# The last tile of a row normalisation: four single row multiplications on VectorE, or one with broadcast factors

## The chip, the cores and the metric

The kernel runs on one core of a Trainium2 chip. The metric is the device time of one execution, in microseconds (us). Before the change it is 316.5 us, the median of three runs (316.45, 316.50, 316.88).

## The reference

The input x has 32 x 512 rows of 1024 fp32 numbers. Each row is divided by the sum of its absolute values:

```python
def reference(x: np.ndarray) -> np.ndarray:
    sums = np.sum(np.abs(x), axis=-1, keepdims=True)
    return (x / (sums + 1e-8)).astype(np.float32)
```

Input and output have 67.1 MB each, so 134.2 MB have to be moved between HBM and the core's memory. Beside that there is little to compute: one reduction and one multiplication for each element.

## The kernel before, in words

The 16384 rows are spread over 128 partitions, 128 rows to each. They are worked off in eleven tiles, numbered 0 to 10. A tile holds R = 12 rows of 1024 numbers for every partition (48 KB a partition, 6144 KB in all), but the last, tile 10, only 8 rows (32 KB a partition, 4096 KB). There are BUFS = 4 buffers; tile i takes the buffer of tile i - 4 once that one is stored.

For every tile the program does four things, in this order:

- `load(i)` (line 87) is a DMA issued on SyncE's queue (SP in the profile; its packets are on q1).
- `normalize` (lines 45 to 73) computes in place. VectorE (DVE) sums the absolute values of all rows in one instruction (line 47), adds 1e-8 (line 54) and takes the reciprocals (line 56): `inv` has one factor for each row. Then the rows are multiplied by their factors, and here the rows are divided among three kinds of instruction. The first `kv` rows go to VectorE in one multiplication of two tensors, where the second is `inv` broadcast along each row (line 58). The next `kt` rows go to VectorE too, one instruction for each row, with the row's factor as a scalar per partition (line 65). The remaining `ks` rows go to ScalarE (ACT), one activation each (line 68).
- `store(i)` (line 97) is a DMA issued on ScalarE's queue (q10). It waits until VectorE's and ScalarE's rows of the tile are done. Tile 0 and tile 8 are stored in two parts, all others in one.
- `load(i + 4)` for the buffer that will come free.

The table `split` on line 76 gives `(kt, ks)` for some tiles; all the others have (0, 0), which means that VectorE does all rows with the one multiplication of line 58. The schedule is manual: each engine carries out its instructions in the order in which the program issues them, and the waits between engines are put in where data or buffers require them.

The end of the program matters here. Tile 9 has (0, 2): ten rows by line 58 on VectorE, two on ScalarE, then its store of 6144 KB. Tile 10 has (4, 4): `kv` is 0, four rows by line 65 on VectorE and four on ScalarE at the same time, then the last store, of 4096 KB. Both stores are cut into packets of a whole partition's rows (`WHOLE`, line 95): 48 KB for tile 9, 32 KB for tile 10. After that only SyncE's final wait for the stores remains.

Of the kernel before, what the change touches and what calls it, by code (L numbers as in the profile page):

```python
# [1 line left out]

# [4 lines left out]

FP32 = mybir.dt.float32
EPS = 1e-8


@with_exitstack
def kernel(
    ctx: ExitStack,
    tc: tile.TileContext,
    x: bass.AP,
    out: bass.AP,
):
    nc = tc.nc
    P = nc.NUM_PARTITIONS  # L20

    x_flat = x.flatten_outer_dims()
    out_flat = out.flatten_outer_dims()
    n, d = x_flat.shape

    R = 12
    BUFS = 4
    HEAD = 32
    per_partition = n // P
    assert n % P == 0 and (per_partition - HEAD) % R == 0  # L30
    rows = [R] * ((per_partition - HEAD) // R + 2) + [HEAD - 2 * R]

    def piece(flat, i):
        head = flat[: P * HEAD, :].rearrange("(p r) d -> p r d", p=P)
        if i < 2:
            return head[:, R * i : R * (i + 1), :]
        if i == len(rows) - 1:
            return head[:, 2 * R :, :]
        a = P * (HEAD + R * (i - 2))
        return flat[a : a + P * R, :].rearrange("(p r) d -> p r d", p=P)  # L40

    sbuf = ctx.enter_context(tc.tile_pool(name="sbuf", bufs=BUFS))
    stats = ctx.enter_context(tc.tile_pool(name="stats", bufs=len(rows)))

    def normalize(x_tile, k, kv, kt):
        s = stats.tile([P, R], FP32)
        nc.vector.tensor_reduce(  # L47
            out=s[:, :k],
            in_=x_tile[:, :k, :],
            axis=mybir.AxisListType.X,  # L50
            op=mybir.AluOpType.add,
            apply_absolute_value=True,
        )
        nc.vector.tensor_scalar_add(out=s[:, :k], in0=s[:, :k], scalar1=EPS)  # L54
        inv = stats.tile([P, R], FP32)
        nc.vector.reciprocal(out=inv[:, :k], in_=s[:, :k])  # L56
        if kv:
            nc.vector.tensor_mul(  # L58
                out=x_tile[:, :kv, :],
                in0=x_tile[:, :kv, :],  # L60
                in1=inv[:, :kv].unsqueeze(2).to_broadcast([P, kv, d]),
            )
        for r in range(kv, kv + kt):
            row = x_tile[:, r, :]
            nc.vector.tensor_scalar_mul(out=row, in0=row, scalar1=inv[:, r : r + 1])  # L65
        for r in range(kv + kt, k):
            row = x_tile[:, r, :]
            nc.scalar.activation(  # L68
                out=row,
                in_=row,  # L70
                func=mybir.ActivationFunctionType.Copy,
                scale=inv[:, r : r + 1],
            )

    last = len(rows) - 1
    split = {0: (3, 4), 1: (0, 3), 2: (0, 3), last - 1: (0, 2), last: (4, 4)}

    tiles = {}

    HALF, WHOLE = 24576, 49152
    FIRST = 3

    def load(i):
        x_tile = tiles[i] = sbuf.tile([P, R, d], FP32, name="x_tile")
        nc.sync.dma_start(out=x_tile[:, : rows[i], :], in_=piece(x_flat, i), max_dma_last_dim=WHOLE if i < 2 else HALF)  # L87

    def store(i):
        if i == 0:  # L90
            parts = [(0, FIRST, 4 * d), (FIRST, R, WHOLE)]
        elif i == last - 2:
            parts = [(0, R // 2, HALF), (R // 2, R, HALF)]
        else:
            parts = [(0, rows[i], WHOLE if i >= last - 1 else HALF)]
        for a, b, size in parts:
            nc.scalar.dma_start(
                out=piece(out_flat, i)[:, a:b, :],
                in_=tiles[i][:, a:b, :],
                max_dma_last_dim=size,  # L100
            )

    def compute(i):
        k = rows[i]
        kt, ks = split.get(i, (0, 0))
        normalize(tiles[i], k, k - kt - ks, kt)

    with tc.manual_schedule():
        for i in range(BUFS):
            load(i)  # L110
        for i in range(len(rows)):
            compute(i)
            store(i)
            if i + BUFS < len(rows):
                load(i + BUFS)


# [1 line left out]
_INS = ['x']  # L119
_OUTS = [((32, 512, 1024), 'float32')]  # L120


# [23 lines left out]
```

## Time and profile before

| what | value |
|---|---|
| time, median of three runs | 316.5 us (316.45 to 316.88) |
| the profiled execution | 316.77 us |
| its span, from the first to the last instruction | 315.2 us |
| VectorE busy | 260.6 us, 83% |
| ScalarE busy | 18.5 us, 6% |
| moved by DMA | 134.22 MB, 426 GB/s over the span |
| line 65 (single rows on VectorE) | 7 instructions, 749 ns each |
| line 58 (broadcast multiplication on VectorE) | 10 instructions of four widths |
| line 68 (single rows on ScalarE) | 16 instructions, 1138 ns each |

All times in the views are counted from the start of the span. The timeline's columns are the start, the duration of the whole group, the engine, the line, the operation, what it writes and reads, the shapes and the number of instructions; a "q" behind an engine's name is its instruction queue, where DMAs are issued. In the groups the columns after the bar are the busy us and the mean ns of one instruction, then the idle time before them. In the windows the columns are the stretch, its length, busy time and instructions of VectorE, ScalarE and GpSimd, the granted clock of TensorE (not used here), the mean busy share of the 16 DMA engines, and GB/s. A packet is counted in the window in which it starts. In the 40 slices each digit is a share in tenths; a slice is 7.9 us.

### The profile page before, as it was taken

How to read it: one execution, taken by the hardware profiler on the slowest of the kernel's cores; microseconds unless marked ns; L12 is line 12 of the kernel's file. 1: busy time of each engine (PE TensorE's matmuls, PEld its weight loads, DVE VectorE, ACT ScalarE, POOL GpSimd, SP SyncE). 2: the span in 40 equal slices, each digit the busy share in tenths (PEclk: the TensorE clock that was granted, in tenths of full speed). 3: DMA queues.
4: the chain of work that ended last, by engine and by line, in shares of the span. 5: the costliest groups of instructions: out<-in, count | busy, mean ns of one | idle time of the engine just before them, and what ended most of it. 6: DMA issues, size and time to landing. Idle time of an engine off the chain costs nothing.

```text
span 315.2 us, 172 instructions
## 1 busy us (share of the span) xinstructions
DVE 260.6 (83%) x50; ACT 18.5 (6%) x17; POOL 0.2 (0%) x4
## 2 busy tenths in 40 slices
DVE  0079999999999999989996997999699969999000
ACT  0010503004000000000000000000000000203200
POOL 0000000000000000000000000000000000000000
DMA  8999999999999999999999999999999999999997
GB/s 318 480 399 412 437 407 464 411 436 413 415 446 437 415 446 437 415 449 434 415 449 437 412 449 437 412 449 437 415 446 437 415 437 434 432 428 496 399 408 324
DMA packets 5761, 134.22 MB, mean 426 GB/s; under 512 B 385, under 2 KB 385, under 8 KB 769
## 3 DMA queue, kind: packets, MB, share of 16 engines
q1 hardware_dynamic: 2736, 67.11, 49.8%
q10 hardware_dynamic: 3024, 67.11, 49.4%
q14 instruction: 1, 0.00, 0.0%
HBM read 67.11 MB, written 67.11 MB: 426 GB/s over the span
## 4 chain that ended last, share of the span: by engine, by line
DVE 40%; DMA 33%; another core or an unknown queue 18%; ACT 1%; issue 0%; SPq 0%
DVE s L47 23%; DMA x_tile<-in_x_dram 17%; DMA out_dram<-x_tile 16%; DVE x_tile L58 15%; ACT x_tile L68 1%; DVE x_tile L65 1%; DVE inv L56 0%; DVE s L54 0%; SPq L87 0%
## 5 line engine op out<-in xcount | busy, mean ns | idle before, releaser
L47 DVE TENSOR_REDUCE s<-x_tile 128x12 f32<-128x12288 f32 (+1 forms) x11 | 138.2, 12562 | 29.8 <-DMA x_tile<-in_x_dram 29.8
L58 DVE TENSOR_TENSOR x_tile<-x_tile,inv 128x12288 f32<-128x12288 f32 (+3 forms) x10 | 113.6, 11358 | 0.5
L68 ACT ACTIVATE x_tile<-x_tile,inv 128x1024 f32<-128x1024 f32 x16 | 17.2, 1138 | 256.9 <-DVE inv L56 256.9
L65 DVE TENSOR_SCALAR x_tile<-x_tile,inv 128x1024 f32<-128x1024 f32 x7 | 4.8, 749 | 0.0
L56 DVE RECIPROCAL inv<-s 128x12 f32<-128x12 f32 (+1 forms) x11 | 2.5, 226 | 0.4
L68 ACT ACT_TABLE_LOAD x1 | 1.3, 1283 | 17.8 <-DMA x_tile<-in_x_dram 17.8
L54 DVE TENSOR_SCALAR s<-s 128x12 f32<-128x12 f32 (+1 forms) x11 | 1.9, 174 | 0.4
L130 POOL MEMSET const-bfloat16-1.0<- 128x1 bf16 x1 | 0.1, 101 | 0.0
L130 POOL MEMSET const-uint8-127<- 128x1 uint8 x1 | 0.1, 101 | 0.0
L130 POOL MEMSET const-float32-0.0<- 128x1 f32 x1 | 0.1, 98 | 0.2 <-issue 0.2
L130 POOL MEMSET const-float32-1.0<- 128x1 f32 x1 | 0.1, 98 | 0.0
## 6 DMA issues: line engine op xcount, KB each, us to landing
x_tile<-in_x_dram SPq DMA_DIRECT2D x10, 6144.0 KB, 36.9
out_dram<-x_tile ACTq DMA_DIRECT2D x8, 6144.0 KB, 49.1
out_dram<-x_tile ACTq DMA_DIRECT2D x2, 3072.0 KB, 33.4
out_dram<-x_tile ACTq DMA_DIRECT2D x1, 4608.0 KB, 37.9
x_tile<-in_x_dram SPq DMA_DIRECT2D x1, 4096.0 KB, 32.2
out_dram<-x_tile ACTq DMA_DIRECT2D x1, 4096.0 KB, 20.9
out_dram<-x_tile ACTq DMA_DIRECT2D x1, 1536.0 KB, 29.3
```

The costliest lines, as they stand in the source:

```text
L47: nc.vector.tensor_reduce(out=s[:, :k], in_=x_tile[:, :k, :], axis=mybir.AxisListType.X, op=mybir.AluOpType.add, apply_absolute_value=True,)
L54: nc.vector.tensor_scalar_add(out=s[:, :k], in0=s[:, :k], scalar1=EPS)
L56: nc.vector.reciprocal(out=inv[:, :k], in_=s[:, :k])
L58: nc.vector.tensor_mul(out=x_tile[:, :kv, :], in0=x_tile[:, :kv, :], in1=inv[:, :kv].unsqueeze(2).to_broadcast([P, kv, d]),)
L65: nc.vector.tensor_scalar_mul(out=row, in0=row, scalar1=inv[:, r : r + 1])
L68: nc.scalar.activation(out=row, in_=row, func=mybir.ActivationFunctionType.Copy, scale=inv[:, r : r + 1],)
L130: nc = _bacc.Bacc("TRN2", target_bir_lowering=False, num_devices=1)
```

## The change

One entry of the table changes: tile 10 has (0, 4) in place of (4, 4).

```diff
-    split = {0: (3, 4), 1: (0, 3), 2: (0, 3), last - 1: (0, 2), last: (4, 4)}
+    split = {0: (3, 4), 1: (0, 3), 2: (0, 3), last - 1: (0, 2), last: (0, 4)}
```

With 8 rows in the tile, `kv` = 8 - 0 - 4 becomes 4 and `kt` becomes 0. So VectorE's four rows of tile 10 are multiplied by one instruction of line 58, over 4096 columns, with the four factors broadcast along the rows, and the four instructions of line 65 over 1024 columns each are gone. ScalarE's four rows, the store and all other tiles are as they were.

## The prediction

> **What bounds the kernel now.** I began with the page: its header, the engines, the 40 slices and the packet total.
>
> ```profile
> span 315.2 us, 172 instructions
> ## 1 busy us (share of the span) xinstructions
> DVE 260.6 (83%) x50; ACT 18.5 (6%) x17; POOL 0.2 (0%) x4
> ...
> DVE  0079999999999999989996997999699969999000
> ...
> DMA  8999999999999999999999999999999999999997
> ...
> DMA packets 5761, 134.22 MB, mean 426 GB/s; under 512 B 385, under 2 KB 385, under 8 KB 769
> ```
>
> VectorE is busy for 83% of the span, but it has slices below 9 and ends three slices (24 us) before the span does. The transfers leave a slice below 9 only at the two ends. 134.22 MB at the 432 GB/s that the DMA view gives for 20:290 is 311 us, out of 315.2. So the bound is the transfers; VectorE matters only where it makes them run dry.
>
> The page's chain of waits names VectorE first (40%). It ends with ScalarE's last activation at 293.22 us and does not follow the store behind it, so it can't say what sets the end. I therefore went to the timeline of the end, where the change lies:
>
> ```profile
> 268.95 10.82 DVE L58 TENSOR_TENSOR x_tile<-x_tile,inv 128x10240 f32<-128x10240 f32 x1
> 279.79 8.69 DVE L47 TENSOR_REDUCE s<-x_tile 128x8 f32<-128x8192 f32 x1
> 279.85 0.34 ACTq L97 DMA_DIRECT2D out_dram<-x_tile  x1
> ...
> 288.96 4.27 ACT L68 ACTIVATE x_tile<-x_tile,inv 128x1024 f32<-128x1024 f32 x4 [17.82 <-DVE inv L56]
> 288.96 2.74 DVE L65 TENSOR_SCALAR x_tile<-x_tile,inv 128x1024 f32<-128x1024 f32 x4
> 293.25 0.34 ACTq L97 DMA_DIRECT2D out_dram<-x_tile  x1
> ```
>
> The four multiplications that the change replaces end at 291.70 (288.96 + 2.74), ScalarE's four rows at 293.23. The last store waits for both and is issued at 293.25: ScalarE's rows release it. What does it meet in its queue? Two answers of the DMA view follow, for 293.6:303.5 and for 303.5:315.2:
>
> ```profile
> DMA packets 80, 3.93 MB, mean 397 GB/s; under 512 B 0, under 2 KB 0, under 8 KB 0
> ...
> q10 hardware_dynamic: 80, 3.93, 91.7%
> ```
> ```profile
> DMA packets 160, 4.19 MB, mean 358 GB/s; under 512 B 32, under 2 KB 32, under 8 KB 32
> ...
> q10 hardware_dynamic: 160, 4.19, 83.1%
> ```
>
> The last store has 4096 KB, which is 4.19 MB: all of it starts after 303.5 us. The 80 packets before are of 3.93 / 80 = 49 KB, the size of the store of tile 9, which was issued at 279.85 and lands 24.6 us later, at 304.5 by the same view. So the last store waits behind tile 9's for about 303.5 - 293.25 = 10.2 us, with its instruction long done. It then takes the rest: the page's row of issues has it land 20.9 us after its issue, at 314.15, and the span ends 1.0 us later.
>
> **The change, part by part.** *Removed:* four multiplications of 128x1024 on line 65, 749 ns each by the page. They start about 0.66 us apart, so together they take 2.74 us, not 4 x 0.749. *Added:* one multiplication of 128x4096 on line 58. The trace has no such width; the groups by form have four others:
>
> ```profile
> L58 DVE TENSOR_TENSOR x_tile<-x_tile,inv 128x12288 f32<-128x12288 f32 x6 | 77.8, 12959 | 0.4
> L58 DVE TENSOR_TENSOR x_tile<-x_tile,inv 128x9216 f32<-128x9216 f32 x2 | 19.5, 9758 | 0.1
> ...
> L58 DVE TENSOR_TENSOR x_tile<-x_tile,inv 128x10240 f32<-128x10240 f32 x1 | 10.8, 10825 | 0.0
> ...
> L58 DVE TENSOR_TENSOR x_tile<-x_tile,inv 128x5120 f32<-128x5120 f32 x1 | 5.5, 5491 | 0.0
> ```
>
> They lie on one line: (12959 - 5491) / 7168 = 1.042 ns per column, and 5491 - 5120 x 1.042 = 157 ns fixed. For 4096 columns that is 4268 + 157 = 4.42 us. As bounds I keep 2.74 us (it costs what the four did) and 5.49 us (no cheaper than the 5120 columns); the line is the nearest, so I take 4.42.
>
> *Moved:* nothing else. Built, the changed program differs in this one place; the other instructions, their order and the two waits of the last store (on VectorE, on ScalarE) are the same.
>
> The sum: VectorE ends at 288.96 + 4.42 = 293.38 in place of 291.70, 1.68 us later. ScalarE's 293.23 covers 1.53 of that, so VectorE now comes last, by 0.15 us. Where VectorE released a store, as tile 9's, the issue came 0.08 us after it (279.77 to 279.85); here it comes 0.02 us after ScalarE. So the last store is issued at about 293.46, 0.21 us later (bounds: 0, and 1.3 with 5.49 us). Nothing is queued behind it on ScalarE, and VectorE has no more work; only SyncE's final wait follows, for the landing.
>
> The cover is the queue. At the start of the kernel the first load is issued at 0.73, and the slices of the DMA view for 0:4 show its packets from about 1.7: 1.0 us from issue to movement. So a last store issued at 293.46 is ready by 294.5, while its turn comes at 303.5: 9 us remain, against 0.21 used. Sum at the end: **0**. With the cover gone it would be +0.21 us, 0.07%, still less than 0.2% (0.63 us), about what a measurement of this kernel can tell from no change.
>
> The profiled execution took 316.77 us, 1.57 outside its span of 315.2; the median of the runs is 316.5, within 0.1% of it. I add the zero to the median.
>
> [...]
>
> **The rivals.** *Slower, by lost transfers.* The two-source multiplication could hold up the DMA engines' reads while it runs, and in a kernel that the transfers bound, each lost us is a us at the end. Windows under VectorE's kinds of work, the last with little else than transfers:
>
> ```profile
> 210.75:223.70 12.95, 12.95 (x1) 0.00 (x0) 0.00 (x0) 1.00 1.00 429
> 239.84:252.80 12.96, 12.96 (x1) 0.00 (x0) 0.00 (x0) 1.00 0.99 429
> 268.95:279.77 10.82, 10.82 (x1) 2.19 (x2) 0.00 (x0) 1.00 1.01 432
> 279.79:288.48 8.69, 8.69 (x1) 0.00 (x0) 0.00 (x0) 1.00 1.02 441
> 291.70:304.00 12.30, 0.00 (x0) 1.52 (x2) 0.00 (x0) 1.00 0.97 421
> ```
>
> The last column is GB/s. Under the multiplication (first three) 429 to 432, under the reduction 441, under neither 421: no order that a hold-up would make, and a window's edge shifts by one round of packets. Priced by the extremes, 20 of 430 GB/s over 4.42 us is 0.2 us. This rival decides from 0.63 us, which needs 14% of the rate lost throughout. At its far end the transfers stop for the added 1.68 us: 318.2 us. For it speaks no row, only that no row has this multiplication beside two stores and no load.
>
> *Faster, by the same door.* If it is the single multiplications that hold up transfers, their going gives some back. Bound: the same 0.2 us, 316.3; at most, if nothing moved in their 2.74 us, 313.8. Against it: in the slices of the DMA view a round of packets starts every 1.8 us in 288.9:293.7, with the multiplications in it, and every 1.8 us in 293.6:303.5, when VectorE is idle. A shorter VectorE stage gives nothing in any case, since ScalarE holds the store to 293.23.
>
> *Slower, by a wait.* VectorE takes the place of ScalarE as what releases the last store. That will happen, and costs 0.21 us of issue; it reaches the end only once the delay exceeds some 9 us, so the multiplication would have to take over 13 us. With a cover that isn't there: 316.7.
>
> *The change doesn't do what it says.* Excluded by the built program: one multiplication of 128x4096 stands where four of 128x1024 stood.
>
> **How the numbers follow.** The hidden delay, 316.5 us: 0.86. The wait with no cover, 316.7: 0.03, also within 0.2%. Lost transfers beyond 0.63 us: 0.07, which includes what I have not thought of and a drift between measurements. Gain beyond 0.63 us: 0.04. So faster 0.04, same 0.89, slower 0.07. The range: the runs of before spread from 316.45 to 316.88; with 0.2 us of the contention bound on both sides and rounded outwards, 316.1 to 317.1.
>
> **What would show it.** In the changed profile: line 65 has three instructions left, the row of 128x4096 on line 58 has 4.42 us, VectorE ends near 293.4 counted as here, the last store is issued about 0.2 us later, its time to landing is shorter by that same amount (20.7 in place of 20.9), its 4.19 MB still start after 303.5, and the span stays within 0.3 us of 315.2. I am wrong if the last store's first packets move with its issue, or if the packets of tile 9's store take longer between 289 and 293.5.

## The result, and the profile after

The changed kernel takes 316.99 us (median of 22 runs, 316.92 to 317.16) against 316.59 us for the kernel before (22 runs, 316.42 to 316.88). The ratio is 1.0012, 95% interval 1.0007 to 1.0018. That is 0.40 us slower: inside the predicted range and inside the 0.2% that I called no change, but a difference that the measurement does tell from nothing. I had forecast zero, so the cause has to be found.

Inside the span the work went as forecast. The page of the changed kernel begins with a span that is shorter than before, not longer (by 0.4 us here, where I had allowed 0.3), and its row of the last store's issue has 20.5 us to landing, where 20.9 stood:

```profile
span 314.8 us, 169 instructions
...
out_dram<-x_tile ACTq DMA_DIRECT2D x1, 4096.0 KB, 20.5
```

The end of its timeline (start, us, engine, line, operation):

```profile
288.80 0.20 DVE L56 RECIPROCAL inv<-s 128x8 f32<-128x8 f32 x1
289.04 4.42 DVE L58 TENSOR_TENSOR x_tile<-x_tile,inv 128x4096 f32<-128x4096 f32 x1
289.04 4.26 ACT L68 ACTIVATE x_tile<-x_tile,inv 128x1024 f32<-128x1024 f32 x4 [17.77 <-DVE inv L56]
293.55 0.34 ACTq L97 DMA_DIRECT2D out_dram<-x_tile  x1
```

The new multiplication takes the 4.42 us that the line through its wider relatives gave. VectorE ends at 293.46 and now releases the last store, 0.09 us later, at 293.55. The DMA view for 293.6:303.3 and for 303.3:315 shows that store in its place behind tile 9's:

```profile
DMA packets 80, 3.93 MB, mean 405 GB/s; under 512 B 0, under 2 KB 0, under 8 KB 0
```
```profile
DMA packets 160, 4.19 MB, mean 358 GB/s; under 512 B 32, under 2 KB 32, under 8 KB 32
```

All 4.19 MB start after 303.3 us. So the late issue did not reach the transfers. The profiled execution, though, took 317.04 us, 2.21 us more than its span (314.83 in the trace); before it was 1.57 to 1.62, by the page's rounded span or the trace's. **The lost time lies outside the span**, where the views of instructions end. The DMA view still shows packets there. These are its slices for 313:318, before and then after (a slice is 0.125 us, each digit a busy share in tenths):

```profile
DMA  0000000000000000000000100000000000000000
...
q14 instruction: 1, 0.01, 0.5%
```
```profile
DMA  0000000000000000000000000000200000000000
...
q14 instruction: 1, 0.01, 0.6%
```

The one visible packet is on q14, which the view calls "instruction" (0.01 MB; 8192 bytes in the trace); I read it as a fetch of instructions. Before, it starts in slice 22, at 315.75 or a little later, 0.6 us after the span's end. After the change it starts in slice 28, near 316.6, 1.8 us after the span's end. And one row of the closing barrier differs in kind. This barrier is the end of the program, where the engines wait for each other (the view of waits has SyncE there twice behind TensorE's queue, 0.6 us in all); EVENT_SEMAPHORE is such a wait, and the columns are its durations in ns (min/median/max), then its first and last start. First the kernel before, then the changed one:

```profile
L141 ACTq EVENT_SEMAPHORE  x2: 17/17/17, 314.5 to 314.9; - x2
L141 DVEq EVENT_SEMAPHORE  x2: 21/21/21, 314.5 to 315.1; - x2
```
```profile
L141 ACTq EVENT_SEMAPHORE  x2: 17/17/17, 314.3 to 314.8; - x2
L141 DVEq EVENT_SEMAPHORE  x2: 21/21/21, 314.3 to 314.8; - x2
```

Before, VectorE's last wait of the program comes 0.2 us behind ScalarE's (315.13 against 314.93 in the trace), with nothing in the program to hold it. After the change both come together. I took this to mean that something holds VectorE at a certain place of its instruction stream, and that the change, which has three VectorE instructions fewer (47 in place of 50, by the page's count of busy ones, without waits and barriers), moved that place.

### The profile page after: what moved, and what is told of

The parts are those of the page before. It is cut to its first block, busy times and chain, and to the rows that moved or that the text cites. A ratio compares the mean times of both kernels' runs of the same rounds, so it can differ in the third digit from the quotient of the medians.

```text
span 314.8 us, 169 instructions
## 1 busy us (share of the span) xinstructions
DVE 262.2 (83%) x47; ACT 18.4 (6%) x17; POOL 0.2 (0%) x4
## 4 chain that ended last, share of the span: by engine, by line
DVE 42%; DMA 33%; another core or an unknown queue 18%; SPq 0%; issue 0%
DVE s L47 23%; DMA x_tile<-in_x_dram 17%; DVE x_tile L58 17%; DMA out_dram<-x_tile 15%; DVE x_tile L65 1%; DVE inv L56 0%; DVE s L54 0%; SPq L87 0%
## 5 line engine op out<-in xcount | busy, mean ns | idle before, releaser
L58 DVE TENSOR_TENSOR x_tile<-x_tile,inv 128x12288 f32<-128x12288 f32 (+4 forms) x11 | 118.0, 10728 | 0.5
L65 DVE TENSOR_SCALAR x_tile<-x_tile,inv 128x1024 f32<-128x1024 f32 x3 | 2.1, 745 | 0.0
## 6 DMA issues: line engine op xcount, KB each, us to landing
out_dram<-x_tile ACTq DMA_DIRECT2D x1, 4096.0 KB, 20.5
```

The source lines that it names most:

```text
L58: nc.vector.tensor_mul(out=x_tile[:, :kv, :], in0=x_tile[:, :kv, :], in1=inv[:, :kv].unsqueeze(2).to_broadcast([P, kv, d]),)
```

## The experiments

**Theory A:** the 0.4 us depend on how many instructions VectorE has in the program, by way of where a fetch of its instructions falls at the end. **Theory B**, the rival: they come from the last tile's work, its later end or its two-tensor form. "Over the span" is the mean of (time - span) over the runs of a kernel; for the kernel before it is 1.63 us throughout, at a mean span of 314.96.

### Count and form taken apart

`after_pad3`: the change, with VectorE's count filled up again.

```diff
+        for j in range(3):
+            nc.vector.memset(pads.tile([P, 1], FP32, name=f"pad{j}"), 0.0)
         for i in range(len(rows)):
             compute(i)
```

> The changed kernel with three one-column memsets on VectorE before the first tile, where VectorE idles for 17.8 us; it has as many VectorE instructions as the kernel before. Theory A (what lies outside the span depends on the number of VectorE instructions in the program: the profiled times are 1.57 us over the span before and 2.2 us after, while the span did not grow): time back at the kernel before, 316.6 us (ratio 1.000), 1.6 us over the span. Theory B (the later end of VectorE in the last tile, or its two-source multiplication, costs the 0.4 us): stays at 317.0 (ratio 1.0013).

Measured: 316.60 us, ratio 1.0001 (0.9992 to 1.0010), 1.64 us over the span. The change is still in it, the loss is gone. VectorE's last wait is late again, by 0.19 us in the trace.

`before_less3`: the last tile as before, three instructions fewer elsewhere.

```diff
+        if eps:
             nc.vector.tensor_scalar_add(out=s[:, :k], in0=s[:, :k], scalar1=EPS)
...
-        normalize(tiles[i], k, k - kt - ks, kt)
+        normalize(tiles[i], k, k - kt - ks, kt, i not in (4, 5, 6))
```

> The kernel before without the addition of 1e-8 in tiles 4, 5 and 6 (left out of the computation there): three VectorE instructions fewer, the last tile as before. Theory A: 317.0 us (ratio 1.0013), 2.2 us over the span, although the last tile is untouched and VectorE has 0.6 us less to do in the middle. Theory B: 316.6 (ratio 1.000).

Measured: 317.01 us, ratio 1.0013 (1.0004 to 1.0021), 2.20 us over the span. The loss is there without the change.

`before_tt4`: the form of the change and a late end, at the old count. In the last tile alone:

```diff
-            nc.vector.tensor_scalar_mul(out=row, in0=row, scalar1=inv[:, r : r + 1])
+            nc.vector.tensor_mul(out=row, in0=row, in1=inv[:, r : r + 1].to_broadcast([P, d]))
```

> The kernel before with the last tile's four single rows multiplied by four two-tensor instructions of 1024 columns with a broadcast factor: the form and the late end of the change (about 4 x 1.2 = 4.9 us, VectorE ending near 293.7, later than in the changed kernel), the number of instructions of before. Theory A: 316.6 us (ratio 1.000), 1.6 us over the span. Theory B: 317.0 or more (ratio 1.0013 or above).

Measured: 316.59 us, ratio 0.9999 (0.9990 to 1.0008), 1.66 us over the span. Its timeline shows that the last tile was even slower than in the change:

```profile
288.86 4.63 DVE L68 TENSOR_TENSOR x_tile<-x_tile,inv 128x1024 f32<-128x1024 f32 x4
288.86 4.26 ACT L71 ACTIVATE x_tile<-x_tile,inv 128x1024 f32<-128x1024 f32 x4 [17.77 <-DVE inv L56]
293.58 0.34 ACTq L100 DMA_DIRECT2D out_dram<-x_tile  x1
```

4.63 us against 4.42, both measured from VectorE's start on the rows, and it costs nothing. Theory B has fallen three times.

### Which place, and in which direction

`before_pad3`: the memsets of above in the kernel before.

> The kernel before with three one-column memsets on VectorE before the first tile: three instructions more. Theory A says that the time over the span changes with the count but not in which direction: if it is one step, the step lies below the count of before and this gives 316.6 (1.6 us over the span); if it falls with each instruction, 316.2. Theory B: 316.6, span and time as before.

Measured: 317.06 us, ratio 1.0015 (1.0006 to 1.0023). Neither of my two readings: more instructions cost as much as fewer. But here the time over the span is 1.79 and the span itself is longer, 315.25 in the mean; its trace has the instruction packet at 292.66 us, within the span, and none after it.

`after_pad2` and `after_pad1`: two memsets and one, in the changed kernel.

> The changed kernel with two memsets on VectorE at the start: one VectorE instruction fewer than before (49 busy ones against 50). Theory A1 (a boundary in VectorE's instruction stream, where an 8 KB instruction packet is fetched, lies at VectorE's very last wait in the kernel before; each instruction fewer moves that boundary out of the span into what follows it): the packet comes later after the span's end than in before, and the time is already that of the change, 317.0 us, 2.2 us over the span. Theory A2 (the cost grows with each missing instruction, 0.4 us / 3 for one): 316.73 us.

> The changed kernel with one memset on VectorE at the start: 48 busy instructions. Theory A1: 317.0 us, 2.2 us over the span. Theory A2: 316.87 us.

Measured: 316.76 us, ratio 1.0007 (0.9998 to 1.0015), 1.96 us over the span; and 316.64 us, ratio 1.0001 (0.9992 to 1.0010), 1.84 us. Both times of theory A1 fail, and so does the straight rise of A2, though its 316.73 was near for two memsets: 49 instructions are dearer than 48. What A1 said of the packet came true: it lies later after the span's end than in the kernel before. What holds is that the place moves, and the cost with it in no simple order. Neither has VectorE's late wait within the span any more; the slices for 313:318, first with two memsets, then with one, have the packet between those of the two kernels:

```profile
DMA  0000000000000000000000200000000000000000
```
```profile
DMA  0000000000000000000000001000000000000000
```

Against the span's end (314.72 and 314.82) it starts 1.1 and 1.2 us later; before it was 0.6, in the changed kernel 1.8.

`before_pad1`: one memset in the kernel before.

> The kernel before with one memset on VectorE at the start: 51 busy instructions. Theory A1: the boundary moves one instruction ahead, before VectorE's last wait; that wait is no longer late (it came 0.19 us after the other engines' in before) and the late instruction is an earlier one of the closing barrier or the fetch lies wholly before it: between 316.4 and 317.1, with the packet earlier against the span's end than in before (0.64 us after it there). Theory A2 in its other direction (each instruction more costs 0.15, as three cost 0.46): 316.75.

Measured: 316.98 us, ratio 1.0010 (1.0001 to 1.0018), 1.79 us over a mean span of 315.17. The closing barrier shows the late instruction one place earlier than in the kernel before; DRAIN is the barrier's instruction ahead of that last wait:

```profile
L145 DVEq DRAIN  x2: 143/1457/2771, 289.1 to 314.8; - x2
L145 ACTq DRAIN  x2: 8/80/152, 293.7 to 314.4; - x2
L145 ACTq EVENT_SEMAPHORE  x2: 17/17/17, 314.3 to 315.1; - x2
L145 DVEq EVENT_SEMAPHORE  x2: 21/21/21, 314.3 to 315.2; - x2
```

VectorE's drain in the barrier starts at 314.8, 0.4 us after ScalarE's, and since the other engines wait for it there, all last waits move to 315.1. One instruction more has moved the hold by one instruction. So this is a place in VectorE's stream. Counted in the trace, waits and barriers included, the late instruction is VectorE's 64th here and in the four kernels with 50 busy ones (the kernel before, `after_pad3`, `before_tt4` and `before_wide4`). In all five the instruction packet starts 0.65 to 0.69 us after the late instruction does, so that instruction was not waiting for this packet.

`before_less11`: all eleven additions of 1e-8 left out, `if eps` with no tile.

> The kernel before without the addition of 1e-8 in all eleven tiles (left out of the computation): 39 busy VectorE instructions, 11 fewer. Theory A1: if the boundary still falls into what VectorE does after the span, 317.0 us; if it has moved behind all of that, no packet after the span and a time below 316.6 (VectorE's late last wait, 0.19 us, gone too: about 316.4). Theory A2: 316.6 + 11 x 0.13 = 318.1 us.

Measured: 316.61 us, ratio 1.0000 (0.9990 to 1.0009), 1.79 us over a mean span of 314.81. No instruction packet comes after the span (slices of 313:318, only the last store's 16 closing packets):

```profile
DMA  0000000000000000000000000000000000000000
...
DMA packets 16, 0.00 MB, mean 0 GB/s; under 512 B 16, under 2 KB 16, under 8 KB 16
## 3 DMA queue, kind: packets, MB, share of 16 engines
q10 hardware_dynamic: 16, 0.00, 0.2%
```

This is the program with no instruction packet at its end, and it is no faster than the kernel before (I had thought of 316.4). So VectorE's late last wait costs the kernel before nothing: it lengthens the span by 0.15 and shortens what follows by 0.16.

### The change with the fetch out of the way, and two controls

`after_less11`: the same omission in the changed kernel.

> The changed kernel without the addition of 1e-8 in all eleven tiles (left out of the computation): 36 busy VectorE instructions. The eleven fewer of the kernel before had no instruction packet after the span, 1.79 us over the span and 316.61 us. Theory A1 (only the place of the fetch counts; the new multiplication is free): no packet after the span, 1.8 us over it, 316.6 us, a ratio within 0.05% of that kernel's. Theory B (the last tile's new form has a price of its own): 317.0.

Measured: 316.60 us, ratio 1.0001 (0.9992 to 1.0010), 1.77 us over the span, no packet after it. Beside the 316.61 of `before_less11`, this is the price of the multiplication itself: none that can be told, 0.01 us between the medians, with intervals of 0.1%.

`after_pool3`: the three memsets on GpSimd (`nc.gpsimd.memset`).

> The changed kernel with three one-column memsets on GpSimd in place of VectorE: the program has as many instructions in all as with three on VectorE, which gave 316.6, but VectorE has 47 busy ones as in the changed kernel. Theory A1 (VectorE's own stream): as the changed kernel, 317.0 us and 2.2 us over the span. Rival (the size of the whole program): 316.6 us.

Measured: 317.06 us, ratio 1.0015 (1.0006 to 1.0024), 2.21 us over the span, where the three on VectorE gave 316.60 and 1.64. It is VectorE's stream that counts here, not the size of the program.

`before_pad16`: sixteen memsets on VectorE.

> The kernel before with sixteen memsets on VectorE at the start: 66 busy VectorE instructions, so that the boundary is crossed well inside the span. Three more gave a packet at 292.66 us, among the last stores' packets, one DMA engine that ended 0.27 us behind the others, and 317.06 us. If an instruction packet among the transfers holds up its DMA engine, which then ends last: the packet near 260 to 290 us, 1.8 us over the span, a span of about 315.2 and 316.9 to 317.1 us. If the rise with three had to do with the end alone: 316.6 us.

Measured: 317.10 us, ratio 1.0017 (1.0008 to 1.0026), 1.80 us over a mean span of 315.30. The packet lies at 244.70 us in the trace, earlier than I expected. Of the last store, one of the 16 closing packets stands alone after 313.7; the DMA view from 313.7 on has for this kernel, and then for `before_less11`:

```profile
DMA packets 1, 0.00 MB, mean 0 GB/s; under 512 B 1, under 2 KB 1, under 8 KB 1
```
```profile
DMA packets 0, 0.00 MB, mean 0 GB/s; under 512 B 0, under 2 KB 0, under 8 KB 0
```

In the trace that engine's data end at 313.99, the other fifteen by 313.58; with three memsets it is 313.87 and 313.60. An engine that carried an instruction packet among its transfers and so comes last would look like this. But the trace of `after_pad3` looks the same, with the last data at 313.91 and the others by 313.55, and its instruction packet starts only at 315.86. So this picture does not show that the packet held an engine up, and why these two spans are longer stays open.

### Where the cover ends

`before_wide4`: the last store released very late, at the old count. In the last tile:

```diff
-            nc.vector.tensor_scalar_mul(out=row, in0=row, scalar1=inv[:, r : r + 1])
+            nc.vector.tensor_mul(out=x_tile[:, :kt, :], in0=x_tile[:, :kt, :],
+                in1=inv[:, :kt].unsqueeze(2).to_broadcast([P, kt, d]))
```

> The kernel before with each of the last tile's four single multiplications replaced by one over all four rows (VectorE's four rows of the last tile are then scaled four times over, so that this part of the output is another): the count of before, but VectorE ends 4 x 4.42 = 17.7 us after 288.96, at about 306.6. The queue covers a late last store until about 302.5 by the prediction's reading (first packets at 303.5, 1.0 us from issue to movement). So the store is issued at 306.7, its packets start at 307.7, 4.1 to 4.2 us late, and the time is 320.7 us. If a late issue costs more than what passes the cover, or the cover is not there: 316.6 + 13.4 = 330.0 us at the most; if it costs nothing at all: 316.6.

Measured: 320.42 us (4 runs), ratio 1.0123 (1.0110 to 1.0137), 1.64 us over the span. Its timeline:

```profile
288.79 4.27 ACT L75 ACTIVATE x_tile<-x_tile,inv 128x1024 f32<-128x1024 f32 x4 [17.79 <-DVE inv L56]
288.79 17.80 DVE L68 TENSOR_TENSOR x_tile<-x_tile,inv 128x4096 f32<-128x4096 f32 x4
306.68 0.34 ACTq L104 DMA_DIRECT2D out_dram<-x_tile  x1
```

Its DMA view for 303:307.4 has 16 packets without data, the closing ones of tile 9's store: the engines are idle here, in the trace until 307.52, 0.84 us after the issue. A store that is issued 13.4 us late (13.6 counted from VectorE's start on the rows) makes the kernel 3.84 us slower, 0.28 less than expected; the rest is covered, 9.6 to 9.8 us. The prediction had some 9 us of cover, which was about right.

## Why the prediction was wrong, point by point

- **The bound** (the transfers; a queue of stores at the end) was right: 4.19 MB after 303.3 us in the changed kernel, and `before_wide4` puts the cover at 9.6 to 9.8 us.
- **The new multiplication**, 4.42 us: measured 4.42.
- **VectorE releases the last store, 0.2 us later:** against VectorE's start on the rows the issue moved from 4.29 to 4.51 us, 0.22 later. To landing it has 20.5 in place of the 20.7 that I named; the end of the profiled span came 0.33 us earlier. Of this 0.19 is VectorE's late last wait, which is gone; the rest is no more than the scatter of the spans (314.7 to 315.0 in the 22 runs).
- **At the end zero:** right for the transfers and for the work. `after_pad3`, `before_tt4` and `after_less11` contain all or part of the change and are within 0.01% of their partners.
- **The step that failed** is the plain one: "The profiled execution took 316.77 us, 1.57 outside its span of 315.2; the median of the runs is 316.5, within 0.1% of it. I add the zero to the median." I took what lies outside the span for a constant. It went from 1.63 to 2.20 us in the mean, while the span went from 314.96 to about 314.8. With it failed "*Moved:* nothing else": three instructions fewer move everything behind them in VectorE's stream. That 316.99 still lies in the range is luck: the range was made of scatter and a bound on contention, and neither made the 0.40 us. (Its lower end has a slip, too: 316.45 less 0.2, rounded outwards, is 316.2, not 316.1.)
- **The rivals** were all about transfers and waits in the last tile. VectorE took ScalarE's place as what releases the last store, as said, and that cost nothing; lost transfers beside the multiplication did not come (tile 9's store, which is under way beside it, landed 24.4 us after its issue; before, 24.6). The 0.40 us belong to none of them.
- **Form and count of VectorE's multiplications:** one of two tensors took 4.42 us, where four of line 65 took 2.74. `before_tt4` tells the two apart: four of two tensors took 4.63 us, so the form added 1.89 us, and one instruction in place of four took off 0.21, or 0.07 for each instruction saved. Neither mattered for the end: `before_tt4` took 316.59 us.

What the trace could have told: the kernel before had VectorE's last wait 0.2 us behind the others with no cause in the program, and an instruction packet 0.6 us after the span. One instruction more (`before_pad1`) moved the late instruction from the last wait to the drain, and three fewer moved the packet from 0.6 to 1.8 us after the span.

VectorE's count against the time, all runs together (busy VectorE instructions, from the page; the packet's start by the trace, counted from the span's end):

| kernel | VectorE | packet, after the span | mean span | over the span | time, median |
|---|---|---|---|---|---|
| `after_less11` | 36 | none | 314.84 | 1.77 | 316.60 |
| `before_less11` | 39 | none | 314.81 | 1.79 | 316.61 |
| the changed kernel | 47 | 1.8 | 314.8 | 2.20 | 316.99 |
| `before_less3` | 47 | 2.0 | 314.78 | 2.20 | 317.01 |
| `after_pool3` | 47 | 1.9 | 314.85 | 2.21 | 317.06 |
| `after_pad1` | 48 | 1.2 | 314.79 | 1.84 | 316.64 |
| `after_pad2` | 49 | 1.1 | 314.84 | 1.96 | 316.76 |
| the kernel before | 50 | 0.6 | 314.96 | 1.63 | 316.58 |
| `after_pad3` | 50 | 0.6 | 315.00 | 1.64 | 316.60 |
| `before_tt4` | 50 | 0.6 | 314.94 | 1.66 | 316.59 |
| `before_pad1` | 51 | 0.3 | 315.17 | 1.79 | 316.98 |
| `before_pad3` | 53 | in the span | 315.25 | 1.79 | 317.06 |
| `before_pad16` | 66 | in the span | 315.30 | 1.80 | 317.10 |

The table's kernels of one count agree within 0.07 us, whatever their last tile does, and from 47 to 66 instructions the packet comes earlier the more VectorE has. None is faster than the kernel before by more than the runs scatter: 316.6 is also what the two kernels without a packet take (316.60 and 316.61).

The views list these packets of 8192 bytes on q14, apart from the data on q1 and q10; for which engine a packet is they do not say. With the packet behind the span, the median time over `before_less11`, which has none, is 0.38 to 0.45 us at 47 instructions, 0.03 at 48, 0.15 at 49, nothing at 50 and 0.37 at 51.

**What stays open.** The trace has no instructions after the span, so which of VectorE's closing instructions is held in the changed kernel, and why its neighbours' hold costs less, is not seen. (The trace of the changed kernel has 61 VectorE instructions, so the 64th would be the third behind the span.) Nor is it seen how the time outside the span is divided between what lies ahead of it and what lies behind it, or what a held instruction waits for: only that the place goes with the count, and the packet with the place. That the packet belongs to VectorE follows from the counts (three memsets on VectorE take the loss away, three on GpSimd do not) and from the late instructions in the barrier, not from a label. Why the two kernels with the packet in mid-run have a longer span (0.44 and 0.49 us over `before_less11`) is not shown.

## What to carry to other kernels

Before a difference of a few tenths of a us is put down to an edit, subtract the span from the time on both sides. A difference found there, as here (1.63 against 2.20 us), speaks against the edit's own work, and a control of the same instruction count settles it (here three idle memsets: 1.64). The control is needed in any case: with 51, 53 and 66 instructions the difference lay in the span, and the count made it all the same. In this program the signs beforehand were an engine's last wait that is late for no reason in the program and an instruction packet close behind the span. And the cover of a store that waited in a queue of stores could be read from the packets' start, here to within 0.8 us: some 9 us read, 9.6 to 9.8 measured.

## What the runs showed of the hardware that I had not expected

- The number of VectorE instructions alone, with no work to speak of in them, moves the time of this program by 0.4 to 0.5 us, with fewer of them and with more: 47 cost 317.0, 50 cost 316.6, 53 cost 317.06.
- An 8 KB instruction packet among the transfers, at 292.66 or 244.70 us, goes with a span 0.3 us longer than before (315.25 and 315.30 against 314.96 in the mean), though the packet itself takes 0.31 us of one of 16 engines (1.3% of their time in 1.5 us). Why is not shown.
- VectorE's hold of 0.19 us at its very last wait costs nothing (the kernel before, 316.58, beside `before_less11`, 316.61); one of 0.4 us at its drain in the barrier, one instruction earlier, costs 0.4 (`before_pad1`, 316.98).
